# A one-core hybrid mLSTM and Hyena layer: the first conditioning round in four quarters instead of two halves, with the query products in pairs of feature tiles

## The chip, the core and the metric

The kernel runs on one core of a Trainium2 chip. The metric is the device time of one execution in microseconds. The kernel before has three timed runs of 1238.62, 1231.26 and 1233.41 us, median 1233.41 us. The execution from which the profile was taken lasted 1238.27 us, and its span, from the first to the last instruction, is 1236.5 us.

## The reference, cut to what matters

One trunk layer is computed for 512 latent tokens and 256 context tokens of 1024 features. A conditioning vector c, one more for the context, is passed through SiLU and multiplied by a matrix of 1024 x 6144. Its first two blocks of 1024 columns are a shift and a scale; they enter the first norm:

```python
mod = (silu_c @ w_ada[l] + b_ada[l])[:, None, :]
sh1, sc1, g1, sh2, sc2, g2 = jnp.split(mod, 6, axis=-1)
h = rmsnorm(x, norm1_g[l]) * (1.0 + sc1) + sh1
hc = rmsnorm(ctx_s, norm1_g[l]) * (1.0 + csc1) + csh1
p = h @ lp["w_in"][:, Q_OFF:] + lp["b_in"][Q_OFF:]
```

Everything else of the layer reads `h` or `hc`: queries, keys, values, gates and three Hyena signals are columns of `h @ w_in`. Independent of them, a small sine network of three layers yields the Hyena filters (`hyena_spectra`), which need a Fourier transform of their own. After that come the mLSTM scan, the long convolutions, the merge, an output projection, a second norm and a SwiGLU.

## The kernel before, in words

Features lie on partitions, in 8 tiles of 128; a matrix product of 32-bit numbers is made of three products, high by high, high by low and low by high (`mm3`, L214 to L217). A number is split by a ScalarE copy to the rounded type (L211 and other lines) and a VectorE subtraction for the rest (L212 and others). The order within an engine is fixed when the program is built: TensorE (PE), VectorE (DVE), ScalarE (ACT) and GpSimd (POOL) each run their own list strictly from the front, and an instruction that waits holds up all that stand behind it on its engine. `tc.issue_after(x)` and `behind()` set where code is put into these lists: behind instruction x, or behind the last gemm.

Only the first 70 us or so are touched. What happens there:

- SyncE (SP) issues all loads in one list, at most eight outstanding: vectors, the network's matrices, x in four pieces, five constant matrices `mats`, then the conditioning matrix and the first weights.
- **The conditioning round** (`ada_slots`, `ada_load`, `ada_first`). The 1024 x 2048 matrix comes in two halves, each of 16 loads of 256 KB. Half 0 holds shift and scale of feature tiles 0 to 3, half 1 those of tiles 4 to 7. A half is 8 (k) times 4 (column groups) products of 128x32 weights `silc` with 256 columns (L319), all four groups side by side in the array; then an ACT copy (L325), two PE transposes (L328), four DVE additions of the bias into `modT` (L335) and one DVE instruction for `amod` (L336). `modT` and `amod` are bias and scale of the next step.
- **The norm of x.** ACT squares and DVE adds up the 8 tiles (L381 to L385), PE sums over partitions (L388), DVE scales (`rv`, L371), POOL raises to -1/2 (L373), PE spreads the result (L375), DVE multiplies each tile of x by it (L1039 for tiles 0 to 3, L1100 for 4 to 7).
- **Modulation** (`modulate`, `modulated`): for each tile ACT writes the high half `hTh` (L1070), DVE writes the same in full (L1075) and subtracts for the low half `hTl` (L1076). It is done for four tiles per half.
- **Query products** (`part(i, p)`): for four query tiles the products over feature tiles 4p to 4p+3, 12 matmuls of 512 columns each, 96 in all. Their weights (`wr`) are loaded and split early (`early_split`, L1046 and L1049).
- **The filter network** (`filter_network`, L401 and L404 on PE, L407 to L412 on DVE, L414 on ACT), the first filter's time values (L445, L446, L447) and its Fourier transform (`filter_spectrum`, 36 matmuls of 256 columns with `dfh` and `dfl`), which needs the splits of `sd` (L212, tile `hb`).
- **The norm of the context**: the same as that of x, with L385 on 256 columns and L1126 for the products.
- After that the first value head (`v_head`, L641 to L643) begins a long stretch in which PE is hardly ever idle.

The line numbers are those of the profile.

## Time and profile before

| what | value |
|---|---|
| timed runs, median (lowest to highest) | 1233.41 us (1231.26 to 1238.62) |
| the profiled execution, its time | 1238.27 us |
| the profiled execution, its span | 1236.5 us |
| PE busy over the span | 1196.6 us |
| first value head begins (L641) | 67.09 us |
| mean granted PE clock | 0.984 |

Times in the views are microseconds from the start of the span. A row of a timeline gives the start, the length, the engine, the line, the operation, the tiles it writes and reads, and in brackets how long the engine had been idle before and who ended that wait. Lengths of instructions that follow each other overlap a little (a DVE instruction of 0.69 us starts its successor after about 0.60), so the distance from start to start is what counts in a chain. In the table by stretches each row gives the length of a stretch, then the busy time of each engine in it with the number of instructions, the granted PE clock as a share of the full one, the busy share of the DMA engines and GB/s. A PE clock below 1 there is a time in which matmuls took twice as long.

### The profile page before, as it was taken

How to read it: one execution, taken by the hardware profiler on the slowest of the kernel's cores; microseconds unless marked ns; L12 is line 12 of the kernel's file. 1: busy time of each engine (PE TensorE's matmuls, PEld its weight loads, DVE VectorE, ACT ScalarE, POOL GpSimd, SP SyncE). 2: the span in 40 equal slices, each digit the busy share in tenths (PEclk: the TensorE clock that was granted, in tenths of full speed). 3: DMA queues.
4: the chain of work that ended last, by engine and by line, in shares of the span. 5: the costliest groups of instructions: out<-in, count | busy, mean ns of one | idle time of the engine just before them, and what ended most of it. 6: DMA issues, size and time to landing. Idle time of an engine off the chain costs nothing.

```text
span 1236.5 us, 16783 instructions
## 1 busy us (share of the span) xinstructions
PE 1196.6 (97%) x6440; PEld 1019.4 (82%) x6440; DVE 835.0 (68%) x1336; ACT 529.4 (43%) x824; POOL 68.2 (6%) x133
## 2 busy tenths in 40 slices
PE   4999999999999999999999988999999999999997
PEld 2799988888888888887788887889888888888886
DVE  6867798978989899796687776756653344332332
ACT  4754455654444544345664543323333223222321
POOL 0011110100010000101001111000000000000000
PEclk9899999999999999999998998999999999999998
DMA  9644452464343443336545647763443332333312
GB/s 355 231 167 149 158 179 86 162 221 137 103 131 116 147 135 128 120 117 227 188 143 173 219 153 244 244 230 119 136 140 100 102 94 94 98 91 97 94 47 69
DMA packets 61137, 183.78 MB, mean 149 GB/s; under 512 B 8440, under 2 KB 12288, under 8 KB 58880
## 3 DMA queue, kind: packets, MB, share of 16 engines
q1 hardware_dynamic: 53552, 153.86, 38.3%
q0 software_dynamic: 7504, 28.84, 6.3%
q8 instruction: 51, 0.84, 0.3%
q14 instruction: 30, 0.25, 0.1%
HBM read 151.74 MB, written 30.93 MB: 148 GB/s over the span
## 4 chain that ended last, share of the span: by engine, by line
PE 90%; DMA 5%; DVE 3%; ACT 1%; issue 1%; POOL 1%; SPq 0%; DVEq 0%; POOLq 0%; ACTq 0%
PE bank L215 27%; PE bank L216 26%; PE bank L217 26%; PE bank L641 2%; PE bank L643 2%; PE bank L642 2%; DMA wr<-in_wph 1%; PE bank L862 1%; PE bank L445 1%; PE bank L598 1%; DMA mats<-in_mats 1%; PE bank L446 1%; DMA hb<-in_dftf 1%; DMA hmd<-s 1%; DMA K<-in_wada 0%
## 5 line engine op out<-in xcount | busy, mean ns | idle before, releaser
L215 PE MATMUL bank<-hTh,wh 128*128 128x512 f32 (+1 forms) x952 | 368.3, 389 | 2.5 <-ACT hTh L1070 2.0
L216 PE MATMUL bank<-hTl,wh 128*128 128x512 f32 (+1 forms) x952 | 367.6, 387 | 2.2 <-DVE hTl L1076 2.2
L217 PE MATMUL bank<-hTh,wl 128*128 128x512 f32 (+1 forms) x952 | 367.0, 386 | 0.0
L211 ACT ACTIVATE wh<-wr 128x1024 fp32r<-128x1024 f32 (+1 forms) x167 | 172.3, 1033 | 434.5 <-PE bank L216 215.5
L212 DVE TENSOR_TENSOR wl<-wr,wh 128x1024 fp32r<-128x1024 f32 (+1 forms) x167 | 198.1, 1189 | 177.6 <-ACT wh L211 176.4
L215 PEld LDWEIGHTS bank<-hTh,wh 128*128 128x128 f32 x952 | 179.8, 189 | 38.0 <-ACT hTh L1070 2.2
L216 PEld LDWEIGHTS bank<-hTl,wh 128*128 128x128 f32 x952 | 179.8, 189 | 37.2 <-DVE hTl L1076 2.5
L217 PEld LDWEIGHTS bank<-hTh,wl 128*128 128x128 f32 x952 | 179.8, 189 | 35.3
L216 PE MATMUL bank<-big,wh 128*128 128x512 f32 (+1 forms) x266 | 95.3, 358 | 0.0
L217 PE MATMUL bank<-big,wl 128*128 128x512 f32 (+1 forms) x266 | 95.0, 357 | 0.0
L215 PE MATMUL bank<-big,wh 128*128 128x512 f32 (+1 forms) x266 | 95.0, 357 | 0.0
L354 DVE SCALAR_TENSOR_TENSOR wr<-wr,crow 128x1024 f32<-128x1024 f32 x32 | 39.0, 1222 | 26.3 <-DMA wr<-in_wada 26.2
L216 PEld LDWEIGHTS bank<-big,wh 128*128 128x128 f32 x266 | 50.8, 191 | 7.2
L215 PEld LDWEIGHTS bank<-big,wh 128*128 128x128 f32 x266 | 50.8, 191 | 7.1
L217 PEld LDWEIGHTS bank<-big,wl 128*128 128x128 f32 x266 | 50.8, 191 | 7.0
L211 ACT ACTIVATE hb<-hb 128x512 fp32r<-128x512 f32 (+1 forms) x49 | 36.7, 768 | 28.5 <-DVE hb L450 18.1
L1514 DVE TENSOR_TENSOR s<-s,bank 128x512 f32<-128x512 f32 x22 | 15.1, 686 | 46.4 <-PE bank L217 46.4
L212 DVE TENSOR_TENSOR hb<-hb,hb 128x512 fp32r<-128x512 f32 (+1 forms) x49 | 40.4, 864 | 2.0 <-ACT hb L211 1.8
L641 PE MATMUL bank<-wh,hTh 128*128 128x256 f32 (+1 forms) x128 | 36.4, 285 | 0.0
L643 PE MATMUL bank<-wh,hTl 128*128 128x256 f32 (+1 forms) x128 | 36.4, 284 | 0.0
L642 PE MATMUL bank<-wl,hTh 128*128 128x256 f32 (+1 forms) x128 | 36.4, 284 | 0.0
L373 POOL TENSOR_TENSOR rr<-rv,negh 128x2 f32<-128x2 f32 (+1 forms) x6 | 5.5, 924 | 514.3 <-DVE rv L371 514.3
(376 smaller groups left out, 2200.8 us busy)
## 6 DMA issues: line engine op xcount, KB each, us to landing
wr<-in_win SPq DMA_DIRECT2D x64, 512.0 KB, 3.7
wr<-in_w SPq DMA_DIRECT2D x60, 512.0 KB, 3.7
wr<-in_wada SPq DMA_DIRECT2D x32, 512.0 KB, 4.7
Kd<-K POOLq DMA_DIRECT2D x8, 1024.0 KB, 4.5
K<-Kd SPq DMA_DIRECT2D x8, 1024.0 KB, 5.7
wr<-in_wv SPq DMA_DIRECT2D x8, 512.0 KB
gmd<-s POOLq DMA_DIRECT2D x16, 256.0 KB, 2.6
wr<-in_wph SPq DMA_DIRECT2D x8, 512.0 KB, 4.4
```

The costliest lines, as they stand in the source:

```text
L211: act.activation(hi, x, AF.Copy)
L212: dve.tensor_sub(lo, x, hi.bitcast(F32))
L215: pe.matmul(o, wh, xh, start=first, stop=False)
L216: pe.matmul(o, wh, xl, start=False, stop=False)
L217: return pe.matmul(o, wl, xh, start=False, stop=last)
L354: dve.scalar_tensor_tensor(w, w, 1.0, crow[:], op0=ALU.mult, op1=ALU.mult, accum_out=s)
L445: pe.matmul(ps[:], lhs, w4h, start=True, stop=False)
L446: pe.matmul(ps[:], lhs, w4l, start=False, stop=True)
L641: pe.matmul(o, xh, wh, start=bool(k == 0), stop=False)
L642: pe.matmul(o, xh, wl, start=False, stop=False)
L643: m = pe.matmul(o, xl, wh, start=False, stop=bool(k == KT - 1))
L1514: dve.tensor_tensor(t[:], t[:], pb[:], op=ALU.mult)
```

## The change: what it does

The conditioning matrix is laid out and loaded in four quarters, each of eight loads of 256 KB, for two feature tiles each. A quarter is 32 products as before but of 128 columns, one ACT copy, one transpose, one DVE addition and one for `amod`. `modulated`, `part` and the product of x with the norm (`norm`) go by pairs of feature tiles. The second stage of the filter network is put ahead of the last square of x. The new order of the main part is written out with `behind()` ahead of quarters 1, 2 and 3, so that each stands behind the query products of the quarter before. On SP, query weights 2 and 3, the first filter's vectors and the Fourier matrix now stand between the quarters. Nothing that is computed differs, and the bytes loaded are the same.

```diff
-    c["wada1"] = w.transpose(4, 0, 3, 2, 5, 1, 6).reshape(2, 4, 2, 128, 4, 256)
+    w = a["w_ada"][0][:, :2048].reshape(KT, 128, 2, 4, 256)
+    c["wada1"] = w.transpose(3, 0, 1, 2, 4).reshape(4, KT, 128, 512)
...
+    def ada_load(part, slots):
+        for k in range(KT):
+            dma(slots[k], I["wada1"][part, k])
...
                 m = pe.matmul(
-                    ps[32 * g : 32 * g + 32, :256], silc[:, k, :], units[k, g], start=bool(k == 0), stop=bool(k == KT - 1)
+                    ps[32 * g : 32 * g + 32, :128], silc[:, k, :], units[k][:, 128 * g : 128 * g + 128],
...
-        copy = act.activation(rows[:, :256], ps[:, :256], AF.Copy)
+        copy = act.activation(rows[:, :128], ps[:, :128], AF.Copy)
         pt = bank()
-        for j in range(2):
-            mark = pe.transpose(pt[:, 128 * j : 128 * j + 128], rows[:, 128 * j : 128 * j + 128], ident)
...
+        mark = pe.transpose(pt[:, :128], rows[:, :128], ident)
...
-                dve.tensor_tensor(o[:, x, y], i[:, x, y], b[:, x, y], op=ALU.add)
+        dve.tensor_tensor(modT[:, 0:2, fs], i, b, op=ALU.add)
...
+    units = [ada_load(0, aslots[0])]
+    load_q(0)
+    units.append(ada_load(1, aslots[1]))
+    load_q(1)
+    for k in range(KT - 1):
         sq_sums(ax_, xt[k], k, 4, PH, "s2", sums)
     next(network)
-    ahead(AH[0])
+    sq_sums(ax_, xt[KT - 1], KT - 1, 4, PH, "s2", sums)
     xb = bank()
     rms_bcast(sums[:, :4], 4, xb, PH, "s2")
     next(network)
...
+    norm(0)
+    *_, (tr, am, copy) = ada_first(0, units[0], PH, "s2")
+    list(early_split(0))
+    qps = [bank(psG) for _ in range(NQ)]
     high, low = modulated(0)
+    part(0, 0)
     with tc.issue_after(high), tc.issue_after(low):
         list(early_split(1))
+    norm(1)
+    part(1, 0)
+    with behind():
+        *_, (tr, am, copy) = ada_first(1, units[1], PH, "s2")
+    load_q(2)
+    units.append(ada_load(2, aslots[2]))
+    load_q(3)
...
+    units.append(ada_load(3, aslots[3]))
...
+    high, low = modulated(1)
+    part(0, 1)
+    with tc.issue_after(high), tc.issue_after(low):
+        list(early_split(2))
+        part(1, 1)
...
+        list(early_split(3))
+        for i in (2, 3):
+            part(i, 0)
+            part(i, 1)
+        norm(2)
+        norm(3)
...
+    with behind():
+        *_, (tr, am, copy) = ada_first(2, units[2], PH, "s2")
+    high, low = modulated(2)
     with tc.issue_after(high), tc.issue_after(low):
+        sp0 = spectrum(*sp.pop(0), (dec, skip, (w4s[:, 0], w4s[:, 1])))
+        next(sp0)
+    for i in range(NQ):
+        part(i, 2)
+    with behind():
+        *_, (tr, am, copy) = ada_first(3, units[3], PH, "s2")
+    high, low = modulated(3)
...
     with tc.issue_after(high), tc.issue_after(low):
-        part(0, 1)
+        split(fh[:], fl[:], fr)
+        part(0, 3)
         csums, cb_ = bank(), bank()
         for k in range(KT):
             sq_sums(ac_, cxt[k], k, 2, PH, "s2", csums)
         next(sp0)
```

Three places in the lists show what moves. In them `[waits ...]` names the engines or DMA queues for which an instruction waits; `bank` is PSUM, `s_` a scratch tile. First DVE, from the end of the filter network on; `hTl` is the low half that PE's products need, `wl` the low half of query weights. Before:

```order
L335 TENSOR_TENSOR modT_78<-bank_284,vecs_69 128x4 [waits PE_49]
L335 TENSOR_TENSOR modT_78<-bank_284,vecs_69 128x4 x3
L336 SCALAR_TENSOR_TENSOR amod_94<-modT_78,vecs_69 128x8 [waits DVE_49]
L1049 TENSOR_TENSOR wl_264<-wr_144,wh_263 128x1024 [waits DMAHW4_49,Activation_49]
L1075 TENSOR_SCALAR s_94_323<-uh_134,amod_94,modT_78 128x512 [waits DVE_49]
L1075 TENSOR_SCALAR s_97_329<-uh_134,amod_94,modT_78 128x512
L1075 TENSOR_SCALAR s_100_335<-ul_136,amod_94,modT_78 128x512
L1075 TENSOR_SCALAR s_103_341<-ul_136,amod_94,modT_78 128x512
L1076 TENSOR_TENSOR hTl_321<-s_94_323,hTh_320 128x512 [waits DVE_49,Activation_49]
```

Now:

```order
L319 SCALAR_TENSOR_TENSOR amod_94<-modT_78,vecs_69 128x4 [waits DVE_49]
L394 SCALAR_TENSOR_TENSOR hb_122<-hb_122 128x512 [waits DVE_49]
L1040 TENSOR_SCALAR s_95_295<-uh_134,amod_94,modT_78 128x512 [waits DVE_49]
L395 TENSOR_SCALAR hb_122<-hb_122 128x512 [waits DVE_49]
L1029 TENSOR_TENSOR wl_285<-wr_144,wh_284 128x1024 [waits DMAHW0_49,Activation_49]
L1041 TENSOR_TENSOR hTl_293<-s_95_295,hTh_292 128x512 [waits DVE_49,Activation_49]
L1040 TENSOR_SCALAR s_98_301<-uh_134,amod_94,modT_78 128x512
L1041 TENSOR_TENSOR hTl_299<-s_98_301,hTh_298 128x512 [waits DVE_49,Activation_49]
L1029 TENSOR_TENSOR wl_311<-wr_145,wh_310 128x1024 [waits DMAHW1_49,Activation_49]
L318 TENSOR_TENSOR modT_78<-bank_357,vecs_69 128x2x4 [waits PE_49]
L319 SCALAR_TENSOR_TENSOR amod_94<-modT_78,vecs_69 128x4 [waits DVE_49]
L1040 TENSOR_SCALAR s_109_390<-ul_136,amod_94,modT_78 128x512 [waits DVE_49]
```

Four low halves were written in a row after one addition to `modT`; now two, and the third stands behind the addition of the next quarter. Then PE at that quarter, in the program now; `hTh_292` and `hTh_298` are feature tiles 0 and 1, `hTh_387` is tile 2:

```order
L217 MATMUL bank_289<-hTh_292,wl_311 128x512 [waits DVE_49]
L215 MATMUL bank_289<-hTh_298,wh_310 128x512
L216 MATMUL bank_289<-hTl_299,wh_310 128x512
L217 MATMUL bank_289<-hTh_298,wl_311 128x512
L305 MATMUL bank_322<-hTh_153,silc_107 32x128 [waits DMAHW1_49,PE_49]
L305 MATMUL bank_322<-hTh_153,silc_107 32x128 x3
...
L314 MATMUL bank_357<-mats_71,s_102_355 128x128 [waits Activation_49]
L215 MATMUL bank_288<-hTh_387,wh_284 128x512 [waits Activation_49]
```

The products of a quarter stand behind the twelve query products of the quarter before, and right behind them come query products that need their result. Last, DVE at the end of the stage; `s_39` collects the context's squares, `hb_419` and `hb_529` are the filter's sums and differences. Before (an excerpt from the last low half on):

```order
L1076 TENSOR_TENSOR hTl_511<-s_137_513,hTh_510 128x512 [waits DMAHW7_49,DVE_49,Activation_49]
L212 TENSOR_TENSOR hb_559<-hb_419,hb_558 128x1024 [waits Activation_49]
L385 TENSOR_TENSOR s_39_133<-s_39_133,s_143_535 128x256 [waits Activation_49]
...
L212 TENSOR_TENSOR wl_697<-wr_695,wh_696 128x1088 [waits DMAHW1_49,DMAHW5_49,PE_49,Activation_49]
L371 TENSOR_SCALAR rv_577<-bank_532 128x2 [waits PE_49]
L212 TENSOR_TENSOR wl_704<-wr_702,wh_703 128x1088 [waits DMAHW6_49,DMAHW2_49,Activation_49]
```

Now:

```order
L1041 TENSOR_TENSOR hTl_603<-s_143_605,hTh_602 128x512 [waits DMAHW3_49,DVE_49,Activation_49]
L212 TENSOR_TENSOR dfl_121<-hb_143,dfh_120 128x1280 [waits DMAHW7_49,Activation_49]
L368 TENSOR_TENSOR s_39_133<-s_39_133,s_149_623 128x256 [waits Activation_49]
...
L212 TENSOR_TENSOR hb_647<-hb_529,hb_646 128x1024 [waits Activation_49] x2
L354 TENSOR_SCALAR rv_659<-bank_620 128x2 [waits PE_49]
L1122 TENSOR_TENSOR K_385<-K_385,bank_621 128x256 [waits DMAHW0_49,PE_49]
...
L212 TENSOR_TENSOR wl_767<-wr_765,wh_766 128x1088 [waits DMAHW5_49,DMAHW1_49,Activation_49]
```

The split of the Fourier matrix (`dfl`) has moved behind the last low half, both filter splits (`hb`) stand ahead of `rv`, and the first split for the value head (`wl`) stands behind the context's products; on PE all four query tiles' last products now stand ahead of the context's sum (L388, now L371) and its spreading (L375, now L358), and the Fourier transform behind them.

More of the change, by code (lines that the diff above doesn't have):

```diff
@@ L1020, in build, with load_q @@
     raws.extend(T(PW, [128, WMAX], F32, "wr") for _ in range(NQ))
-    slots = [ada_slots(PH, i) for i in range(2)]
-    units = [ada_load(PH, 0, slots[0])]
-    ada = ada_first(PH, 0, units[0], "s2")
-    def ahead(n):
-        for _ in range(n):
-            m = next(ada)
-        return m
-    for k in range(KT):
+    aslots = [ada_slots(PH, i) for i in range(4)]
+    units = [ada_load(0, aslots[0])]
+    def load_q(i):
+        dma(raws[i][:, :1024].rearrange("p (a b) -> p a b", a=KT), I["win"][FT_Q + i])
+    load_q(0)
+    units.append(ada_load(1, aslots[1]))
+    load_q(1)
+    for k in range(KT - 1):
         sq_sums(ax_, xt[k], k, 4, PH, "s2", sums)
     next(network)
-    ahead(AH[0])
+    sq_sums(ax_, xt[KT - 1], KT - 1, 4, PH, "s2", sums)
     xb = bank()
@@ L1036, in build @@
     next(network)
-    ahead(AH[1])
-    for k in range(4):
-        dve.tensor_tensor(xt[k], xt[k], xb[:], op=ALU.mult)
     early = []
@@ L1049, in early_split @@
         dve.tensor_sub(hl[1], raw, hl[0].bitcast(F32))
-    e0 = early_split(0)
-    with tc.issue_after(next(e0)):
-        tr, am, copy = ahead(8 - AH[0] - AH[1])
-    with tc.issue_after(am):
-        list(e0)
-    dec, skip = spectrum_vectors(PH, *sp[0])
-    dma(w4r, I["hw4"][sp[0]].rearrange("p f n -> p (f n)"))
-    for i in range(1, NQ):
-        dma(raws[i][:, :1024].rearrange("p (a b) -> p a b", a=KT), I["win"][FT_Q + i])
-    dma(fr, I["dftf"])
-    units.append(ada_load(PH, 1, slots[1]))
-    t = T(PH, [128, KT, CTX], F32, "K")
-    dma(t[:], I["cxT"])
-    for k in range(KT):
-        cxt.append(t[:, k])
     hT = ([], [])
```

88 lines of the change are left out of this document (32 added, 56 removed).

## The prediction

> **What bounds the kernel now.** First the chain that ended last, by engine, and the table by stretches, cut where PE's first low product (L216) and the first value head (L641) begin.
>
> ```profile
> PE 90%; DMA 5%; DVE 3%; ACT 1%; issue 1%; POOL 1%; SPq 0%; DVEq 0%; POOLq 0%; ACTq 0%
> ```
>
> ```profile
> 0.00:31.13 31.13, 12.56 (x92) 7.20 (x92) 20.03 (x50) 13.02 (x20) 1.32 (x6) 0.99 0.95 355
> 31.13:67.09 35.96, 35.96 (x213) 28.55 (x214) 32.08 (x55) 26.77 (x43) 0.70 (x1) 0.92 0.70 236
> 67.09:1236.50 1169.41, 1148.10 (x6138) 983.66 (x6136) 782.86 (x1234) 489.61 (x763) 66.16 (x126) 0.99 0.43 140
> ```
>
> PE ends 90% of the chain. It is filled completely from 31.13 to 67.09 (35.96 of 35.96 us), and behind the value head for 1148.1 of 1169.41. The change touches nothing behind 67.09, so I take what the value head's start moves for what the end moves. Ahead of 31.13 PE has 12.56 us of work and 18.57 of idleness: that is what an earlier start can win, and every wait put into the full stretch behind it is lost. Then PE's timeline around those two marks:
>
> ```profile
> 15.00 1.87 PE L388 MATMUL bank<-mats,s 128*128 128x1 f32 x8 [7.87 <-DVE s L385]
> 19.73 1.34 PE L375 MATMUL bank<-mats,rr 128*128 128x128 f32 x8
> 21.56 1.13 PE L404 MATMUL bank<-hb,hb 128*128 128x256 f32 x4
> 23.31 2.10 PE L319 MATMUL bank<-K,silc 128*32 128x256 f32 x31
> 28.41 0.49 PE L215 MATMUL bank<-hTh,wh 128*128 128x512 f32 x1 [2.01 <-ACT hTh L1070]
> 31.13 0.80 PE L216 MATMUL bank<-hTl,wh 128*128 128x512 f32 x1 [2.23 <-DVE hTl L1076]
> 44.01 1.07 PE L319 MATMUL bank<-hTh,silc 128*32 128x256 f32 x16
> 62.88 0.28 PE L215 MATMUL bank<-hb,dfh 128*128 128x256 f32 x1
> 67.09 0.28 PE L641 MATMUL bank<-wh,hTh 128*128 128x272 f32 x1
> ```
>
> The early idle time ends at a low half from DVE (2.23 us the last piece). Half 1 starts at 44.01 without a wait: nothing stands in brackets, so its loads had landed, and the query products behind it covered its way through ACT and DVE.
>
> **The change, part by part.** Prices of DVE and ACT come from these rows; where DVE's instructions follow each other, the distance from start to start counts.
>
> ```profile
> 25.52 0.38 ACT L325 ACTIVATE s<-bank 128x256 f32<-128x256 f32 x1 [2.94 <-PE bank L319]
> 25.15 0.69 DVE L410 SCALAR_TENSOR_TENSOR hb<-hb 128x512 f32<-128x512 f32 x1
> 26.94 0.36 DVE L335 TENSOR_TENSOR modT<-bank,vecs 128x4 f32<-128x4 f32 x4
> 27.42 1.22 DVE L1049 TENSOR_TENSOR wl<-wr,wh 128x1024 fp32r<-128x1024 f32 x1
> 28.56 1.00 DVE L1075 TENSOR_SCALAR s<-uh,amod,modT 128x512 f32<-128x512 f32 x2
> 30.38 2.50 DVE L1076 TENSOR_TENSOR hTl<-s,hTh 128x512 fp32r<-128x512 f32 x4
> 43.42 1.48 DVE L212 TENSOR_TENSOR dfl<-hb,dfh 128x1280 fp32r<-128x1280 f32 x1
> 48.82 0.37 DVE L335 TENSOR_TENSOR modT<-bank,vecs 128x4 f32<-128x4 f32 x4 [1.32 <-PE bank L328]
> 49.43 1.52 ACT L1070 ACTIVATE hTh<-uh,modT,amod 128x512 fp32r<-128x512 f32 x2 [1.30 <-DVE amod L336]
> 54.98 3.07 DVE L385 TENSOR_TENSOR s<-s,s 128x256 f32<-128x256 f32 x6
> 57.97 1.22 DVE L212 TENSOR_TENSOR hb<-hb,hb 128x1024 fp32r<-128x1024 f32 x1
> 17.23 1.01 POOL L373 TENSOR_TENSOR rr<-rv,negh 128x4 f32<-128x4 f32 x1 [16.39 <-DVE rv L371]
> 60.88 0.70 POOL L373 TENSOR_TENSOR rr<-rv,negh 128x2 f32<-128x2 f32 x1 [42.65 <-DVE rv L371]
> ```
>
> *A quarter's products.* Half 1 and products of 128 columns with few weight columns stand in the trace so (the first row is one of the chain):
>
> ```profile
> 44.08 3.59 PE bank L319 x64
> ```
>
> ```profile
> 187.17 0.38 PE L771 MATMUL bank<-mats,hb 128*8 128x128 f32 x2
> 187.39 0.38 PE L770 MATMUL bank<-mats,hb 128*8 128x128 f32 x2
> ```
>
> The 64 records of a half take 3.59 us, 224 ns per four side by side. A pair of narrow ones goes in 187.39 − 187.17 = 0.22, so 0.11 each; 16 fours of a quarter make 1.75 us. That is an estimate for the floor, since those narrow ones don't run four abreast: a quarter might cost as much as a half if a record can't be issued faster than its 56 ns (3.59), and hardly less than 1.75. I take 1.75, as a four now has half the columns. The Trainium skill, "TensorE: Matmul & The Clock Gate", section "Wait — 56ns, not 53.3ns?", gives two floors for small matmuls, 25 ns from start to start, and 62 ns where decoding in hardware is off. By the first a quarter would be 1.6, by the second 4.0; the trace's 56 ns already stands below the second, so it speaks for the first.
>
> *The start.* The sums of x end about 0.5 us later, as the second network stage goes in front of them, and the third network layer is still ahead; then quarter 0 needs 1.75 at full clock and up to 3.5 at half instead of 3.59. Adding up from 15.00: sums to 15.00 + 1.87 + 0.5 = 17.4, DVE and POOL (1.01 and the handing over) to 18.8, L375 (1.34) to 20.15, the third layer (L404, 1.13) to 21.3, quarter 0 to about 23.9, its copy and transpose to 24.7 (25.52 to 26.94 before, and those four additions are now one). DVE has then two 0.7s of the network and one shorter operation (like L1075, 0.46), one L1075 of 0.46 and the `wl` split of 1.14 ahead of the first low half (0.62). The first low product starts at about 28.95 instead of 31.13: **−2.2**. If DVE's network part is late by what it now starts later, this is 0; it can't be better than −3.5, for the chain of the norm stays.
>
> *One more quarter behind it.* Quarters 1 to 3 are 3 × 1.75 = 5.25 against 3.59: **+1.7**.
>
> *The gap behind quarter 1.* Twelve query products, eleven of them from 28.95 on, end at about 33.7 (half clock; 32 at full). Quarter 1 then runs until 36.1. Behind it stand products that need its result, and in DVE's list the addition to `modT` of this very quarter comes right behind the `wl` split that the twelve need: the low halves of tiles 2 and 3, the norms of the rest and the network's stack are queued behind `modT`, which waits for PE. The way back is: copy and transpose to `modT` about 0.75 (48.82 − 47.67 = 1.15 for the wide one, end of L319 being 44.08 + 3.59), addition and `amod` 0.27, two L1075 of 0.46, one L1076 of 0.62, together 2.55. One high product of 0.23 fits in (38.10 to 38.33 below). PE waits **+2.3**. Bounds: 1.0 if the first low half comes right behind the first L1075 and the copy overlaps, 3.2 with the wide half's 1.15 and the 0.6 that lie between its addition and L1070.
>
> *Behind quarter 2.* The eight L445/L446 (of the shape of a query product, 0.23 each) are issued there and cover 1.84 of the 2.55, a high product 0.23: **+0.4**, between 0 and 1.2.
>
> ```profile
> 38.10 0.23 PE bank L215
> ...
> 59.70 0.49 PE bank L388 x4
> ...
> 61.69 0.66 PE bank L375 x4
> ```
>
> *Behind quarter 3.* PE's list now goes straight to the last 24 query products, which need tiles 6 and 7: **+2.3** again, same bounds.
>
> *The context's sum.* Call T the end of quarter 3. DVE then has, one behind the other: the way back and L1075 until T + 2.0, two low halves 1.25, `dfl` 1.41 (it ran at 43.42, ahead of half 1, before), seven additions of the context 7 × 0.51 = 3.57, two filter splits of 1.14; POOL 0.7 and PE's spreading 0.46 follow, which with `rv` and the handing over (0.7 in all) is T + 12.3. Query products end at T + 2.55 + 23 × 0.23 = T + 7.8. The sums (L388, 0.49) and the spreading take 0.95 of the 4.5 between; **+3.6** of idle PE, where before PE had query products and the Fourier transform at hand. Bounds: 2 if ACT's squares come early enough that the additions overlap nothing else, 5 if `dfl` also waits for ACT's `dfh`. The value head's splits (1.14 each) arrive while the 36 transform matmuls run (67.09 − 62.88 = 4.2), just in time.
>
> *Loads.* The bytes stay, and 32 loads of 256 KB remain 32. A quarter of 2 MB takes about 5.9 us at the 355 GB/s of the first 31 us. Before, all of half 1 had landed by 44.01; quarter 3 is wanted only at some 56. Query weights 2 and 3 and the Fourier matrix, now behind quarter 1 on SP, are used 10 us and more after. Nothing: 0, and at worst 2 if quarter 1 itself were late by its place behind the query weights.
>
> *The clock.* PE's granted clock in stretches with gaps:
>
> ```profile
> 30.00:35.00 5.00, 3.87 (x9) 3.13 (x10) 4.94 (x9) 4.96 (x8) 0.00 (x0) 0.54 1.05 386
> 711.00:717.00 6.00, 3.51 (x13) 2.92 (x13) 5.45 (x10) 2.52 (x3) 0.00 (x0) 0.72 0.46 148
> 737.00:741.00 4.00, 3.87 (x32) 3.87 (x33) 1.33 (x5) 1.80 (x4) 0.00 (x0) 1.00 0.91 286
> 649.00:659.00 10.00, 10.00 (x40) 8.22 (x40) 5.79 (x21) 4.94 (x14) 2.89 (x4) 0.53 0.55 177
> ```
>
> ```profile
> 713.53 0.76 PE L215 MATMUL bank<-uh,K 128*128 128x512 f32 x1 [2.49 <-DVE dx L924]
> 737.13 0.44 PE L966 MATMUL bank<-mats,hs 128*128 128x128 f32 x2 [1.73 <-DVE hs L959]
> ```
>
> After the idle time of the first 30 us the clock falls to 0.54, and the products there run in twice the time; the change keeps that. A gap of 2.49 us was followed by 0.72 over 6 us, a loss of 1.7; one of 1.73 by no loss. Two of the new gaps (2.3 behind quarter 1, 3.6 at the context's sum) lie at or above the former: 2 × 1.7 = **+3.4**, between 0 and 9.4 (0.47 × 10 us for each, as in 649 to 659). A fall behind quarter 3 costs nothing, as DVE sets the end there.
>
> *Sum.* −2.2 + 1.7 + 2.3 + 0.4 + 2.3 + 3.6 + 3.4 = +11.5 us. The profiled execution has 1236.5 us of span and 1.8 around it, 1238.3 together, and lies 4.9 above the median of the runs; its like would come to 1249.8, and on the median of 1233.4 the change makes **1244.9**.
>
> **Rivals.**
> 1. *The early start carries through.* If the gaps are covered after all (ACT's copy quicker, low halves made in the shade of products), only the first term stays: 1233.4 − 2.2 = 1231.2, not slower. For it: PE has 18.57 idle us ahead, and every low half costs DVE but 0.62. Against it: DVE's list has `modT` of the next quarter ahead of all work that could cover it. It decides if PE's wait behind quarter 1 is under half a microsecond.
> 2. *The gaps come, but the clock stays.* Without the 3.4: 1241.5. For it: after 1.73 us it stayed at 1.00. Against it: 2.49. The Trainium skill, same page, section "Why this matters for your kernels", asks for no idle gap beyond some 3 us, and "What's actually happening" puts the window at about 3.4; by that rule most of these gaps do no harm, but 2.49 us did here.
> 3. *A narrow product costs as much as a wide one.* Then each of quarters 1 to 3 is 1.84 longer and quarter 0 as well: 4 × 1.84 = 7.4 more, 1252.3. For it: 56 ns per record could be the issue and not the columns. Against it: the 0.11 us of the narrow pairs.
> 4. *The clock stays down long.* As in 649 to 659, 4.7 per gap instead of 1.7: 6.0 more, 1250.9. For it: two gaps 20 us apart; against it: single gaps here cost a short time.
>
> **How the numbers follow.** The forecast has 0.37, the first rival 0.08, the second 0.30, the third 0.10, the fourth 0.15. The likeliest gives 1244.9, its own range by the bounds of the gaps is 1240 to 1250. The range for all is 1234 to 1254: it leaves out the first rival and the far ends. One per cent is 12.3 us, about what a measurement of this kernel can tell from no change: slower begins at 1245.7. Of the forecast 0.45 lies above it (0.17), of the third 0.09, of the fourth 0.13, of the second 0.03: slower 0.42. Faster needs less than 1221.1, which a few of the first rival's cases reach: 0.03. Same 0.55.
>
> **What the profile after would show.** Right: first low product near 29; DVE idle for 3 to 6 us ahead of the addition to `modT` of quarter 1; PE waits of about 2 behind quarters 1 and 3 and of nearly 4 ahead of the context's spreading; the 64 records of a quarter in about 1.8 us; a value head near 75 to 79. Wrong: PE full from 29 on, quarters of 3.6 us, or a PE wait on a conditioning load.

## The result, and the profile after

| | before | after |
|---|---|---|
| timed runs, median (lowest to highest) | 1233.93 us (1230.92 to 1238.62), 6 runs | 1245.41 us (1242.64 to 1247.0), 6 runs |
| ratio after/before, 95% interval | | 1.0082 (1.0057 to 1.0107) |
| profiled execution, span | 1236.5 us | 1244.1 us |
| first low product (L216) begins | 31.13 us | 30.28 us |
| Fourier transform (L215 with `dfh`) begins | 62.88 us | 74.12 us |
| PE's next wait, at the same instruction (L738, now L721) | 185.74 us | 199.42 us |

The median rose by 11.5 us, 0.9%; 1244.9 was predicted. The value head's first matmuls are at 79.33 us, but 12 of the transform's matmuls now stand behind them, so the transform and the wait near 200 us are the better marks.

PE's timeline of the changed kernel, only rows with a wait and the quarters' products (L305) between them; the bracket says how long PE was idle before and for whom.

```profile
18.62 2.07 PE L358 MATMUL bank<-mats,rr 128*128 128x128 f32 x8 [1.46 <-POOL rr L356]
20.49 1.91 PE L387 MATMUL bank<-hb,hb 128*128 128x256 f32 x4
22.33 1.08 PE L305 MATMUL bank<-hTh,silc 128*32 128x128 f32 x16
...
27.95 0.74 PE L215 MATMUL bank<-hTh,wh 128*128 128x512 f32 x1 [1.78 <-ACT hTh L1035]
30.28 0.79 PE L216 MATMUL bank<-hTl,wh 128*128 128x512 f32 x1 [1.59 <-DVE hTl L1041]
...
37.52 0.33 PE L314 MATMUL bank<-mats,s 128*128 128x128 f32 x1 [0.46 <-ACT s L312]
39.16 0.73 PE L215 MATMUL bank<-hTh,wh 128*128 128x512 f32 x2 [1.30 <-ACT hTh L1035]
...
50.22 0.33 PE L314 MATMUL bank<-mats,s 128*128 128x128 f32 x1 [0.40 <-ACT s L312]
...
60.39 0.33 PE L314 MATMUL bank<-mats,s 128*128 128x128 f32 x1 [0.55 <-ACT s L312]
62.02 1.97 PE L215 MATMUL bank<-hTh,wh 128*128 128x512 f32 x4 [1.30 <-ACT hTh L1035]
...
70.13 0.61 PE L371 MATMUL bank<-mats,s 128*128 128x1 f32 x4 [0.77 <-DVE s L368]
73.25 1.22 PE L358 MATMUL bank<-mats,rr 128*128 128x128 f32 x4 [2.51 <-POOL rr L356]
```

Where the kernel before had no idle PE at all (31.13 to 67.09), there are now seven waits: 0.46 + 1.30 behind quarter 1, 0.40 behind 2, 0.55 + 1.30 behind 3, 0.77 + 2.51 at the context's sum; 7.3 us. DVE shows the other side of the first, what ended just ahead of quarter 3's addition, and how the last comes about:

```profile
31.40 1.22 DVE L1029 TENSOR_TENSOR wl<-wr,wh 128x1024 fp32r<-128x1024 f32 x1
37.89 0.17 DVE L318 TENSOR_TENSOR modT<-bank,vecs 128x8 f32<-128x8 f32 x1 [5.28 <-PE bank L314]
...
59.43 0.41 DVE L434 TENSOR_TENSOR hb<-hb,fs 1x256 f32<-1x256 f32 x1
...
63.87 1.49 DVE L212 TENSOR_TENSOR dfl<-hb,dfh 128x1280 fp32r<-128x1280 f32 x1 [0.47 <-ACT dfh L211]
...
67.00 3.08 DVE L368 TENSOR_TENSOR s<-s,s 128x256 f32<-128x256 f32 x6 [1.30 <-ACT s L367]
69.99 2.35 DVE L212 TENSOR_TENSOR hb<-hb,hb 128x1024 fp32r<-128x1024 f32 x2
72.26 0.15 DVE L354 TENSOR_SCALAR rv<-bank 128x2 f32<-128x2 f32 x1
```

DVE stood still for 5.28 us with two low halves, the remaining norms and the network's stack behind the addition to `modT`. At the end `dfl`, the seven additions, both filter splits and `rv` run one behind the other, and only then can POOL and PE's spreading follow. PE and DVE wait for ACT's copy of a quarter's result (L312), its high halves and its squares. ACT was itself held up twice: by a load of filter vectors ahead of quarter 3's copy, and by PE ahead of six of the context's squares, where it copies the first query tile out of PSUM (the evacuation, L1057):

```profile
59.55 0.63 ACT L408 ACTIVATE fd<-fd 128x512 f32<-128x512 f32 x1 [3.15 <-DMA fd<-in_hdec]
60.08 0.26 ACT L312 ACTIVATE s<-bank 128x128 f32<-128x128 f32 x1
...
65.97 0.69 ACT L1057 ACTIVATE cx<-bank,vecs 128x512 f32<-128x512 f32 x1 [1.52 <-PE bank L217]
```

The chain of the changed kernel gives a quarter's price, and three stretches the clock:

```profile
47.94 1.93 PE bank L305 x64
```

```profile
35.00:62.00 27.00, 22.96 (x264) 17.80 (x263) 17.68 (x31) 13.82 (x22) 0.00 (x0) 1.00 0.58 205
62.16:65.58 3.42, 3.42 (x9) 2.65 (x10) 2.95 (x4) 2.29 (x4) 0.00 (x0) 0.50 0.00 0
72.40:79.23 6.83, 5.98 (x28) 5.98 (x29) 4.74 (x12) 3.78 (x5) 0.70 (x1) 0.50 0.00 0
```

Behind quarter 1 the clock stayed up; it fell for 3.42 us behind quarter 3 and for 6.83 us at the context's sum.

From the first low product to the wait near 200 us the kernel before took 185.74 − 31.13 = 154.6 us, this one 199.42 − 30.28 = 169.1: 14.5 more. Waits are 7.3 of it, one more quarter 3 × 1.93 − 3.59 = 2.2, and the clock some 4 (half speed in 62.16 to 65.58 and 72.40 to 79.23 is 5.1 us, less 0.4 of it that fell on idle time and 0.7 that the time right behind the first low product lost less than before, 2.3 for 3.0; its row for the kernel before is the next view). About one microsecond I can't assign.

```profile
31.13:37.21 6.08, 6.08 (x14) 4.84 (x15) 6.02 (x9) 6.03 (x9) 0.00 (x0) 0.50 1.02 369
```

The spans of the two profiled executions differ by 7.6 only. The kernel before happened to have a stretch at half clock far behind the change:

```profile
648.00:659.00 11.00, 11.00 (x46) 9.22 (x45) 6.79 (x25) 5.94 (x16) 3.05 (x4) 0.53 0.58 191
```

That costs 0.47 × 11 = 5.2 us, and 648 to 672 of the changed kernel is at 1.00. Of the twelve profiled executions in this document eight have such a stretch of 10.2 us or more between 648 and 673, whatever the edit, and four have none. Single executions therefore can't be subtracted at the end of the span. What can be compared is time × clock, the time of a run multiplied by its mean granted clock: 1242.64 × 0.989 and 1247.0 × 0.986 agree within 0.6 us though the times differ by 4.4. Time × clock is 1228.9 on average over the six runs after (0.9872 the mean clock), and 1220.7, 1220.0 and 1220.2 over the 23, 19 and 23 runs of the kernel before beside the experiments (0.990, 0.988, 0.989). So of the 11.5 us some 8.6 are waits and work; the rest, about 3, is clock (by the mean clocks 1.1 to 3.3). It is a rough measure, since a wait at half clock counts half.

### The profile page after: what moved, and what is told of

It reads as the page before. It is cut to its first block, busy times and chain, and to the rows that moved or that the text cites. A ratio compares the mean times of both kernels' runs of the same rounds, so it can differ in the third digit from the quotient of the medians.

```text
span 1244.1 us, 17042 instructions
## 1 busy us (share of the span) xinstructions
PE 1197.3 (96%) x6568; PEld 1022.4 (82%) x6568; DVE 834.3 (67%) x1334; ACT 529.3 (43%) x826; POOL 68.2 (5%) x133
## 3 DMA queue, kind: packets, MB, share of 16 engines
q0 software_dynamic: 7504, 28.84, 6.3%
## 4 chain that ended last, share of the span: by engine, by line
PE 87%; DMA 5%; DVE 3%; ACT 2%; issue 1%; POOL 1%; SPq 0%; DVEq 0%; POOLq 0%; ACTq 0%
PE bank L215 26%; PE bank L216 26%; PE bank L217 25%; PE bank L626 2%; PE bank L625 2%; PE bank L624 2%; DMA wr<-in_wph 1%; PE bank L581 1%; PE bank L845 1%; DMA hb<-in_hw 1%; PE bank L428 1%; DMA K<-in_wada 1%; DMA hmd<-s 1%; DMA hTh<-in_wada 1%; DVE wl L212 1%
## 5 line engine op out<-in xcount | busy, mean ns | idle before, releaser
L215 PE MATMUL bank<-hTh,wh 128*128 128x512 f32 (+1 forms) x952 | 369.2, 390 | 5.9 <-ACT hTh L1035 4.4
L216 PE MATMUL bank<-hTl,wh 128*128 128x512 f32 (+1 forms) x952 | 368.3, 388 | 1.7 <-DVE hTl L1041 1.6
L215 PEld LDWEIGHTS bank<-hTh,wh 128*128 128x128 f32 x952 | 179.9, 190 | 41.7 <-ACT hTh L1035 5.0
L216 PEld LDWEIGHTS bank<-hTl,wh 128*128 128x128 f32 x952 | 179.8, 189 | 37.7 <-DVE hTl L1041 3.1
L216 PE MATMUL bank<-big,wh 128*128 128x512 f32 (+1 forms) x266 | 95.4, 359 | 0.0
L215 PE MATMUL bank<-big,wh 128*128 128x512 f32 (+1 forms) x266 | 95.1, 358 | 0.0
L216 PEld LDWEIGHTS bank<-big,wh 128*128 128x128 f32 x266 | 50.9, 191 | 7.2
L215 PEld LDWEIGHTS bank<-big,wh 128*128 128x128 f32 x266 | 50.8, 191 | 7.2
```

Of the source, the lines that this page charges most:

```text
L215: pe.matmul(o, wh, xh, start=first, stop=False)
L216: pe.matmul(o, wh, xl, start=False, stop=False)
```

## The experiments

All but the last four are the changed kernel with one edit. Time × clock is the mean over the runs. The ratio is to runs of the kernel before that were taken alongside, with medians of 1233.02 to 1234.54 us. The times of the first low product and of the transform, and the distance from the first low product to PE's wait near 200 us, are those of one profiled execution each, so they hold its clock too.

| run | runs | median us | ratio to before (95%) | time × clock | first low | transform | to wait near 200 |
|---|---|---|---|---|---|---|---|
| after | 6 | 1245.41 | 1.0082 (1.0057 to 1.0107) | 1228.9 | 30.28 | 74.12 | 169.1 |
| q1_early | 9 | 1240.92 | 1.0068 (1.0043 to 1.0092) | 1225.3 | 30.03 | 68.43 | 163.0 |
| q3_early | 6 | 1245.35 | 1.0088 (1.0056 to 1.0120) | 1228.9 | 29.50 | 71.07 | 166.0 |
| squares_first | 8 | 1244.60 | 1.0096 (1.0069 to 1.0124) | 1228.4 | 28.84 | 71.94 | 167.6 |
| filled_gap | 9 | 1241.46 | 1.0083 (1.0053 to 1.0112) | 1229.9 | 29.94 | 71.88 | 164.9 |
| net_behind_sums | 4 | 1247.44 | 1.0106 (1.0082 to 1.0130) | 1229.7 | 31.08 | 74.58 | 168.0 |
| warm_start | 4 | 1246.29 | 1.0097 (1.0076 to 1.0118) | 1227.4 | 27.79 | 71.11 | 168.7 |
| q1_early_filled | 10 | 1238.16 | 1.0026 (1.0003 to 1.0049) | 1225.6 | 30.50 | 69.12 | 161.6 |
| quarters_covered | 10 | 1233.07 | 1.0001 (0.9984 to 1.0019) | 1224.1 | 28.92 | 63.21 | 157.1 |
| windows_first | 12 | 1235.94 | 1.0016 (0.9995 to 1.0037) | 1224.8 | 30.10 | 65.14 | 161.6 |
| windows_first_warm | 12 | 1238.93 | 1.0051 (1.0026 to 1.0076) | 1224.8 | 28.51 | 63.64 | 160.2 |

**q1_early.** `ada_first` is cut into its products and its finish.

```diff
     norm(0)
     *_, (tr, am, copy) = ada_first(0, units[0], PH, "s2")
+    with tc.issue_after(tr):
+        ps1 = ada_products(1, units[1])
...
-    part(0, 0)
+    with behind():
+        part(0, 0)
     with tc.issue_after(high), tc.issue_after(low):
-        list(early_split(1))
+        *_, wl1 = early_split(1)
+        with behind(), tc.issue_after(wl1):
+            tr, am, copy = ada_finish(1, ps1, PH, "s2")
     norm(1)
-    part(1, 0)
-    with behind():
-        *_, (tr, am, copy) = ada_first(1, units[1], PH, "s2")
+    with tc.issue_after(tr):
+        part(1, 0)
```

> The changed kernel with quarter 1's products issued right behind quarter 0's, in the time in which PE waits for the first low halves, and its copy, transpose and addition behind the first six query products. My theory (a quarter's way back through ACT and DVE, with nothing on PE to cover it, is lost time that carries to the end): the 1.8 us of PE waits behind quarter 1 and its 1.95 us of products leave the full stretch, the Fourier transform begins at about 70.4 instead of 74.12 us, and the median falls by 3.7 to about 1241.7. Rival (narrow products or DVE's throughput set the pace, the wait only shows them): the transform begins within 1 us of 74.1. Rival (clock): a change of a multiple of 1.7 us that follows a fall of the granted clock and not the waits.

PE's and DVE's rows of this kernel:

```profile
30.03 0.50 PE L216 MATMUL bank<-hTl,wh 128*128 128x512 f32 x1 [1.80 <-DVE hTl L1046]
31.29 0.79 PE L216 MATMUL bank<-hTl,wh 128*128 128x512 f32 x1 [0.29 <-DVE hTl L1046]
...
43.05 0.65 PE L305 MATMUL bank<-hTh,silc 128*32 128x128 f32 x16
```

```profile
31.15 1.22 DVE L1034 TENSOR_TENSOR wl<-wr,wh 128x1024 fp32r<-128x1024 f32 x1
32.76 0.17 DVE L320 TENSOR_TENSOR modT<-bank,vecs 128x8 f32<-128x8 f32 x1 [0.39 <-PE bank L316]
```

DVE's 5.28 us have become 0.39, PE has no wait above 0.35 us between 31.3 and 45.4, and quarter 2 begins at 43.05 instead of 47.87. Time × clock fell by 3.6 (3.7 expected for the median), the median by 4.5. The intervals of the two ratios overlap, the single runs' time × clock don't (1223.5 to 1226.7 here, 1227.7 to 1229.6 in the changed kernel). The transform begins at 68.43, 2 us earlier than expected; a shorter wait at the context's sum (0.23 instead of 0.77) and less time at half clock ahead of it are part of that. So this much of the loss was the wait and the quarter's products in the full stretch, not narrow products or DVE's throughput.

**q3_early.**

```diff
-    for i in range(NQ):
-        part(i, 2)
-    with behind():
-        *_, (tr, am, copy) = ada_first(3, units[3], PH, "s2")
+    part(0, 2)
+    part(1, 2)
+    with behind():
+        ps3 = ada_products(3, units[3])
+    with behind():
+        part(2, 2)
+    with behind():
+        tr, am, copy = ada_finish(3, ps3, PH, "s2")
+    with tc.issue_after(tr):
+        part(3, 2)
```

> The changed kernel with quarter 3's products, transpose and addition ahead of the last two query tiles' products over tiles 4 and 5. My prediction's term by itself says that the 2.3 us wait behind quarter 3 goes and that DVE's chain starts 2.7 us earlier: transform at 71.4, median −2.7. The trace of the changed kernel speaks for a rival: DVE's filter windows and sums end only at 59.84 and an ACT operation that waits for a load only at 60.1, so the addition to modT can't come before 59.9 whatever PE does; then the transform begins only 0.9 us earlier, at 73.2, and the wait behind quarter 3 moves to PE's first product with tile 6.

Time × clock did not move (1228.9), nor the median. DVE and ACT in this kernel:

```profile
58.25 0.41 DVE L439 TENSOR_TENSOR hb<-hb,fs 1x256 f32<-1x256 f32 x1
58.58 0.15 DVE L320 TENSOR_TENSOR modT<-bank,vecs 128x8 f32<-128x8 f32 x1
...
59.04 0.63 ACT L413 ACTIVATE fd<-fd 128x512 f32<-128x512 f32 x1 [2.59 <-DMA fd<-in_hdec]
59.57 1.50 ACT L1040 ACTIVATE hTh<-ul,modT,amod 128x512 fp32r<-128x512 f32 x2
```

The addition to `modT` follows the filter's sums without a wait for PE: DVE's list was the bound for it, as the second theory says. For the high half that PE waits for, ACT's load wait was: `amod` was written at 58.92, and the high half began only at 59.57, behind the instruction that waited for the load. PE's wait with tile 6 shrank from 0.55 + 1.30 to 1.24, and the one for the context's sum grew from 0.77 to 1.18. The 2.7 us that the term by itself would give did not come. (The transform begins 3.05 us earlier because the first low product is 0.8 earlier and less time was at half clock: here it did not fall behind quarter 3.)

**squares_first.**

```diff
-        part(0, 3)
         csums, cb_ = bank(), bank()
-        for k in range(KT):
+        for k in range(KT - 1):
             sq_sums(ac_, cxt[k], k, 2, PH, "s2", csums)
+        part(0, 3)
+        sq_sums(ac_, cxt[KT - 1], KT - 1, 2, PH, "s2", csums)
```

> The changed kernel with six of the context's eight squares on ACT ahead of the first query tile's evacuation, which waits for PE. Theory of the trace after (an evacuation that waits for PE holds up ACT, hence DVE's additions, by 1.3 us): the additions run without that wait, the transform begins 1.0 us earlier, at 73.1. Theory as predicted (DVE's list alone, one instruction behind the other): no change, 74.1.

DVE in this kernel:

```profile
63.29 1.49 DVE L212 TENSOR_TENSOR dfl<-hb,dfh 128x1280 fp32r<-128x1280 f32 x1 [0.47 <-ACT dfh L211]
64.70 3.60 DVE L368 TENSOR_TENSOR s<-s,s 128x256 f32<-128x256 f32 x7
68.21 2.35 DVE L212 TENSOR_TENSOR hb<-hb,hb 128x1024 fp32r<-128x1024 f32 x2
```

The 1.30 us wait inside the additions is gone: `dfl` to filter splits takes 4.92 us instead of 6.12. PE's waits at the sum fell from 3.28 to 2.35. Time × clock fell by 0.5, less than the spread of these runs; that the order makes the wait possible is shown, its worth in time isn't. The order alone does not make it: in the profiles of filled_gap and warm_start, where the clock did not fall behind quarter 3, the additions run without that wait in the old order.

**filled_gap.**

```diff
...
-        rms_bcast(csums[:, :2], 2, cb_, PH, "s2")
+        spare = bank()
+        with tc.issue_after(csum):
+            for _ in range(6):
+                fill = pe.matmul(spare[:], early[0][0][:, 0], hT[0][0][:], start=True, stop=True).ins
+        with tc.issue_after(fill):
+            rms_bcast(csums[:, :2], 2, cb_, PH, "s2")
```

> The changed kernel with six matmuls of 512 columns, whose results nobody reads, between the context's sum and its spreading, where PE is idle for 2.5 us. If the idle time makes the clock fall there (72.40 to 79.23 at half in the changed kernel), the fall is at least one window of 3.41 us shorter and the mark 120 us further on (PE's wait at 198.9) comes 1.5 to 3 us earlier, with the transform still at 74.1. If the clock falls for another reason (the kinds of matmul, the time): no change. If the six are in the way: up to 1.4 later.

The same stretch, 72 to 80 us, in this kernel:

```profile
72.00:80.00 8.00, 8.00 (x69) 8.00 (x68) 7.84 (x14) 7.04 (x14) 0.00 (x0) 1.00 0.28 86
```

in the kernel before it in this list, squares_first:

```profile
72.00:80.00 8.00, 8.00 (x56) 8.00 (x55) 7.78 (x14) 5.40 (x10) 0.00 (x0) 0.79 0.29 84
```

and in the changed kernel:

```profile
72.00:80.00 8.00, 6.75 (x34) 6.75 (x35) 5.91 (x13) 4.65 (x7) 0.70 (x1) 0.57 0.08 12
```

Matmuls that compute nothing wanted kept the clock up: here and in q1_early_filled the clock is full behind the sum, and in all six profiles that leave PE idle there for more than 2.3 us (after, q1_early, q3_early, squares_first, net_behind_sums, warm_start) half clock follows. The distance to the wait near 200 us is 4.2 us shorter, but 1.7 of it is not the edit's: behind quarter 3, ahead of the six matmuls, the clock stayed up in this execution. And whole runs don't settle what it is worth: five of nine lie between 1240.0 and 1241.5 (clock 0.990 to 0.993), four between 1244.8 and 1248.8 (0.983 to 0.988), and the ratio is that of the changed kernel. The two groups lie some 6 us apart, and a stretch at half clock like the one near 650 us is worth 5; that it is what parts them is not shown.

**q1_early_filled**, both edits at once.

> Both edits of q1_early (median −4.5 us against the changed kernel) and of filled_gap (−4.0). If the wait behind quarter 1 and the clock behind the context's gap are two separate losses, they add up: the median is 1237 (±1.5), half-clock time between the first low product and PE's wait at 199 is one window at most. If both were the same loss (the clock): not below 1240.

1238.16: within the 1.5 us, and below the 1240 of one and the same loss, so the median speaks for two losses that add up. It doesn't show it, as the −4.0 for filled_gap is itself not settled by whole runs; and the distance to the wait near 200 us is 7.5 us shorter than in the changed kernel, not 6.1 + 4.2. Two windows at half clock were left ahead of the wait near 200 us, 31.67 to 35.09 and 58.98 to 62.39, where one at most was expected.

**net_behind_sums**

```diff
-    for k in range(KT - 1):
+    for k in range(KT):
         sq_sums(ax_, xt[k], k, 4, PH, "s2", sums)
     next(network)
-    sq_sums(ax_, xt[KT - 1], KT - 1, 4, PH, "s2", sums)
```

> The changed kernel with the filter network's second stage back behind the sums of x. Prediction's view (the sums of x are held up half a microsecond by it and everything behind follows): L371 at 15.0 instead of 15.30, first low product 0.3 to 0.5 earlier at best; but the network's third layer is then later. Rival (the move is what brought the start forward by 0.85 at all): the first low product is 0.8 or more later. In the median nothing above 1 us either way.

```profile
15.29 1.87 PE L371 MATMUL bank<-mats,s 128*128 128x1 f32 x8 [8.23 <-DVE s L368]
...
22.08 2.08 PE L387 MATMUL bank<-hb,hb 128*128 128x256 f32 x4 [1.43 <-ACT hb L397]
```

The sums of x begin at 15.29 as with the move (15.30), so the move costs them nothing; the third layer, which waits 1.43 us for the second, begins at 22.08 instead of 20.49, and the first low product is 0.8 later. That speaks for the rival: the move brings the start forward, by about what the change gained there. It is one execution, and the clock's return differs from one to the next by more than 0.8 us; the wait of 1.43 and time × clock, 0.8 higher, point the same way.

**warm_start**

```diff
-    sq_sums(ax_, xt[KT - 1], KT - 1, 4, PH, "s2", sums)
...
+    first = fill(10)
+    with tc.issue_after(first):
+        xsum = sq_sums(ax_, xt[KT - 1], KT - 1, 4, PH, "s2", sums)
+    with tc.issue_after(xsum):
+        second = fill(5)
     xb = bank()
-    rms_bcast(sums[:, :4], 4, xb, PH, "s2")
-    next(network)
+    with tc.issue_after(second):
+        rms_bcast(sums[:, :4], 4, xb, PH, "s2")
+        next(network)
```

> The changed kernel with ten and five small matmuls, whose results nobody reads, in PE's idle time ahead of the sums of x and ahead of the norm's spreading. If the start missed its predicted 2.2 us because the clock stayed at half until 24.6 us (spreading 2.07 instead of 1.34 us, third layer 1.91 instead of 1.13, quarter 0 2.9 instead of 1.95), these run at full clock now and the first low product begins 1.0 to 2.0 us earlier, at 28.3 to 29.3. If DVE's network part decides: no change, 30.3.

```profile
19.22 1.03 PE L388 MATMUL bank<-hb,hb 128*128 128x256 f32 x4
...
26.73 0.79 PE L215 MATMUL bank<-hTh,wh 128*128 128x512 f32 x1 [3.81 <-ACT hTh L1048]
27.79 0.79 PE L216 MATMUL bank<-hTl,wh 128*128 128x512 f32 x1 [0.27 <-DVE hTl L1054]
```

The third layer's four records take 1.03 us instead of 1.91, and the first low product begins 2.5 us earlier, more than expected and 1.05 us ahead of the earliest one without such matmuls (28.84, squares_first). The half clock was what the start had lost. In time nothing came of it (1246.29, four runs): time × clock is 1.5 lower, but ahead of the first high product PE was now idle for 3.81 us, and from 25.09 to 31.91 the clock was at half again.

**quarters_covered** keeps the quarters and the pairs and moves them (on top of q1_early's and squares_first's edits):

```diff
         part(1, 1)
+        with behind():
+            ps2 = ada_products(2, units[2])
+        norm(2)
...
+        with behind():
+            part(2, 0)
+            part(2, 1)
...
+        with behind():
+            tr, am, copy = ada_finish(2, ps2, PH, "s2")
+        with tc.issue_after(tr):
+            part(3, 0)
+            part(3, 1)
...
+        split(fh[:], fl[:], fr)
         next(sp0)
-    for i in range(NQ):
-        part(i, 2)
+    with behind():
+        ps3 = ada_products(3, units[3])
+    with behind():
+        part(0, 2)
+        part(1, 2)
+    with behind():
+        tr, am, copy = ada_finish(3, ps3, PH, "s2")
+    with tc.issue_after(tr):
+        part(2, 2)
+        part(3, 2)
```

> All four quarters kept, but each quarter's products are issued ahead of query products that don't need it (1 behind 0, 2 ahead of the last two query tiles' products over tiles 0 to 3, 3 ahead of those over 4 and 5), the split of the Fourier matrix is made behind the low halves of tiles 4 and 5, six context squares come ahead of the first evacuation, and the context's sum goes between the last query products. My theory (the change costs by waits that nothing covers, and by the clock that falls behind them, not by quarters as such): PE's waits behind the quarters and at the context's sum fall from 7.3 to under 2 us, the transform begins at 60.5 to 62.5 (before: 62.88), and the median is within 2 us of the kernel before, or up to 3 below it. Rival (four narrow quarters cost 2.3 us more of PE and DVE's list is as long as the stage): the transform begins at 64 to 66 and 3 us or more of the loss stay.

PE's waits of this kernel from 26 to 76 us, by who is waited for (us in total, times, longest):

```profile
PE bank L216 <- DVE hTl L1046: 2.1, 2, 1.8
PE bank L363 <- POOL rr L361: 1.4, 1, 1.4
PE bank L305 <- DVE hb L435: 1.3, 1, 1.3
PE bank L376 <- DVE s L373: 0.6, 1, 0.6
```

```profile
22.00:62.00 40.00, 34.17 (x368) 25.99 (x368) 35.61 (x64) 24.85 (x40) 1.61 (x1) 1.00 0.75 268
```

No wait for ACT's copy or for a high half is left, the waits behind the first low product are 3.5 us instead of 7.3 (under 2 were expected), and the clock is full throughout. The transform begins at 63.21 (60.5 to 62.5 were expected), and PE's wait near 200 us comes at 186.05, before at 185.74. The median is 1233.07 beside 1233.56 of the kernel before, ratio 1.0001 (0.9984 to 1.0019, so within some 2 us): the loss is gone with all four quarters in place. Time × clock says how: it is 4.8 below the changed kernel but still 4 above the kernel before, and the clock, 0.992 on average against 0.988, or 4.7 us, makes up for that. Of these, 3.0 are the stage's own in the profiled executions: before, PE ran at half clock from 31.13 to 37.21, and here it didn't. The remaining 1.7 lie behind the stage and may be chance.

**windows_first** and **windows_first_warm**: the Fourier matrix split behind the filter's windows (`split(fh[:], fl[:], fr)` after `next(sp0)`), and the same with warm_start's matmuls.

> As quarters_covered, with the Fourier matrix split behind the filter's windows instead of ahead of them. In quarters_covered quarter 3's products wait 1.3 us for a PSUM bank that the windows free (VectorE's first one came after the split of the Fourier matrix on ScalarE). If that is so the wait goes, the median falls by 1 to 1.5 us to about 1231.8, and this version is 1 to 2 us faster than the kernel before. Rival (VectorE's list is as long as the stage, so the wait moves to the context's sum or to the value head's weights): median 1233 again.

> As windows_first, with the fifteen small matmuls of warm_start at the start. There the first low product came 2.5 us earlier, but the time ahead of it was idle for 3.8 us and the clock fell again; here quarter 1's products fill that idle time. If the early start is worth its 2 us once nothing behind it waits: 2 us below windows_first, about 1230. If VectorE sets the pace from the first low half on and was early by as much: also 2 us. If the loss returns as a wait at the context's sum or as a clock window: within 1 us of windows_first.

The profiled execution of windows_first is the slowest of its twelve. In it PE no longer waits for the bank (the products of quarter 3 begin at 47.41 without a wait), but there is a new wait in the value head:

```profile
77.42 0.76 PE L629 MATMUL bank<-wh,hTh 128*128 128x272 f32 x4 [1.86 <-ACT wh L211]
```

The rival holds as far as one execution shows: the wait has moved to the value head's weights, and neither version is faster than the kernel before (1.0016 and 1.0051). The early start was lost too: with it the transform begins 1.5 us earlier, time × clock is the same, 1224.8, and the median is 3 us higher, which none of the expectations has; why the clock is lower there (0.988 for 0.991) stays open.

## Why the prediction was right

The mechanism was right: a quarter's way through ACT and DVE, with nothing on PE to cover it, and the clock that falls behind such waits. The sum was 8.1 us of waits and work and 3.4 of clock; the runs show about 8.6 and 3. Term by term:

- **The start, −2.2**: −0.85 in this execution. What the prediction had wrong is the step from the spreading (1.34) to quarter 0: it took durations of the kernel before, where products of half 0 stood ahead of the spreading and kept PE busy. With these moved, the spreading takes 1.87 from start to start, the third layer 1.84, quarter 0 3.0. From `modT` on (26.21 to 30.28) it took 4.07 us where 4.25 were worked out. warm_start shows that half clock was the cause. In squares_first, with the same instructions up to there, the third layer's records took 1.58 instead of 1.91 and the first low product came at 28.84, so this term differs between executions by 1.4 us. That the sums of x would end half a microsecond later was wrong as well (15.30, as without the move).
- **One more quarter, +1.7**: 2.2, since a quarter takes 1.93 us, not 1.75. The rival of products as dear as wide ones (3.59) is out.
- **Behind quarter 1, +2.3**: 1.76, and q1_early shows that it is lost time. DVE's list stood still in the way described, but the way back that PE waited for is another: the sum went on to DVE's low half, and PE's last wait (1.30) ended with ACT's high half; the two high products behind it covered the low half. (Its 36.1 for the end of quarter 1 doesn't follow from 33.7 and 1.75 either; no term uses it.)
- **Behind quarter 2, +0.4**: 0.40, by luck. The 0.4 was what the filter's eight products and a high product would leave uncovered. They covered all of that (no wait from 50.32 to 52.73), and the 0.40 is PE's transpose, which stands ahead of them, waiting for ACT's copy.
- **Behind quarter 3, +2.3**: 1.85 of waits, but the cause is half right only: DVE's filter windows and sums ended just ahead (59.84), and ACT's copy stood behind a load, so an earlier quarter 3 brings nothing (q3_early).
- **The context's sum, +3.6**: 3.28, and the chain of `dfl`, additions, splits and `rv` is the predicted one. It missed 1.3 us in which ACT's squares stand behind an evacuation that waits for PE (squares_first).
- **The clock, +3.4**: some 4 in the profiled execution and about 3 in the runs, but wrong in place. It was priced for two gaps "at or above" 2.49 us, and the 2.3 behind quarter 1 is not; there the clock didn't fall here (in squares_first it did, below). At the context's sum it fell for 6.83 us, twice the priced time. "A fall behind quarter 3 costs nothing" wasn't tried by itself, but the traces speak against it: from `dfl` to `rv` DVE took 8.39 us here (63.87 to 72.26) and 7.19 in filled_gap (63.23 to 70.42) and in warm_start (62.05 to 69.24), which have the same order and no fall there. Of the 7.3 us of waits some are thus the clock's.
- **Loads, 0**: no PE wait on a load appears behind 30 us. But ACT waited 3.15 us for a later filter's vectors, loaded into the buffer `fd` that the windows had just read, and quarter 3's copy stood behind that instruction: it came 0.24 us after the end of the products (59.84 to 60.08).

The rivals: the early start did not carry through, the clock did not stay up, quarters did not cost like halves, and no gap cost 4.7 us of clock (1.7 behind quarter 3, 3.4 at the sum, less the idle part). The total is closer than its terms deserve, and that is luck: a start 1.3 us too good and waits about 1.3 us too long cancelled.

## What to carry to other kernels

Cutting a step into more pieces, each with a way through three engines and back, costs nothing only if the piece's consumers are not the next thing in the producer's list: put other work of the same engine between, as quarters_covered does, or the way back is paid once per piece. Here it gained nothing even so (1.0001). Look in each engine's list for what stands behind the instruction that waits: here one addition to `modT` held up two low halves, the norms and the stack for 5.3 us. And price an operation at the clock that will be granted there, not the one in the old row: where work ahead of it is moved away, it may run at half clock (the third layer's records, 1.91 us instead of 1.13).

## What the runs showed of the hardware that was not expected

The granted clock changes on a fixed grid in each execution: 62.16, 65.58, 72.40 and 79.23 lie 3.41, 6.83 and 6.83 us apart. In all twelve profiles the stretches at half clock, but for the one at the very end, are multiples of 3.41 us long. So I count PE's idle time within each window of the grid. The waits of 0.46 and 1.30 us behind quarter 1 were followed by full clock in the changed kernel (35 to 62 above, at 1.00), where they lie in two windows (0.87 us idle in 34.85 to 38.27, 0.94 in the next), and by one window at half in squares_first, where they lie in one (1.47 us idle in 35.24 to 38.65):

```profile
35.35 0.33 PE L314 MATMUL bank<-mats,s 128*128 128x128 f32 x1 [0.46 <-ACT s L312]
36.98 0.73 PE L215 MATMUL bank<-hTh,wh 128*128 128x512 f32 x2 [1.30 <-ACT hTh L1035]
```

```profile
38.65:42.06 3.41, 3.41 (x10) 2.64 (x9) 3.38 (x4) 3.37 (x6) 0.00 (x0) 0.50 1.08 415
```

How the gap lies to the grid does not decide it alone, though. In net_behind_sums 1.77 us lie in one window, and the next is at full clock:

```profile
37.28:40.70 3.42, 1.65 (x50) 1.19 (x42) 1.21 (x4) 1.16 (x3) 0.00 (x0) 1.00 1.09 402
40.70:44.11 3.41, 3.35 (x14) 2.44 (x15) 3.15 (x6) 3.41 (x5) 0.00 (x0) 1.00 1.00 389
```

Counted over the twelve profiles, half clock followed each of the 32 windows at full clock with more than 1.8 us of idle PE, 20 of the 61 with 1.0 to 1.8 us, and one of the some 4000 with less. What decides between 1.0 and 1.8 us stays open.

The Trainium skill, "TensorE: Matmul & The Clock Gate", section "What's actually happening", describes a free-running window of about 3.4 us, and the trace agrees with 3.41. In "Why this matters for your kernels" it asks for no idle gap beyond some 3 us; here 1.47 us in one window were enough once, more than 1.8 each time, and the measurement decides.

Runs of one program spread with the clock in the same way (1227.96 to 1237.82 us in 23 runs of the kernel before, at clocks of 0.994 and 0.986), which is why time × clock, with a standard deviation of 0.8 to 1.0 us in the kernel before, shows an edit of 3 us better than the time does.
